# Two attentions of a decoder trunk: raw input for the first, forget gates earlier in the second, and weight low parts added by transfers

## The chip, the cores and the metric

The kernel runs on one core of a Trainium2 chip. The metric is the device time of one execution in microseconds (us); lower is better. Engines are named as the profile names them: PE (TensorE), PEld (its weight loads), DVE (VectorE), ACT (ScalarE), POOL (GpSimd), SP (SyncE). Each engine works through its own queue of instructions strictly in order; a transfer (DMA) is issued by SP or by POOL and runs on 16 shared DMA engines.

## The reference, cut to what matters

The residual stream `x` has 512 tokens of 1024 numbers, 16 heads of 64. There are two layers; each is an attention, a SwiGLU feed-forward and a gated per-layer embedding. Layer 0 uses stick-breaking attention, layer 1 softmax attention with a cumulative forget-gate bias.

```python
def rms_norm(x, g):
    y = xf * lax.rsqrt(jnp.mean(xf * xf, axis=-1, keepdims=True) + EPS)
    return y * g
# layer 0
hn = rms_norm(h, attn_norm_g[0])
q, k, v = split(hn @ sb_w_qkv)
z = einsum('bhqd,bhkd->bhqk', q, k) * scale
w = exp(log_sigmoid(z) + later)      # later: sum of -softplus(z) over the keys between
h = h + merge_heads(w @ v) @ sb_w_o
# layer 1
hs = rms_norm(h, shared_norm_g)
kvf = hs @ shared_w_kvf              # keys, values, 16 forget-gate columns
f_logit = kvf[..., 2 * HD:] + shared_b_f
f_cum = cumsum(log_sigmoid(f_logit), axis=1)
logits = q_normed @ k_normed * scale + f_cum[query] - f_cum[key]
```

The factor of `rms_norm` that belongs to a token (`r` below) can be put in after a product instead of before it, since it is one number for each token.

## The kernel before

**Numbers.** Every float32 operand of a product is held as two `float32r` tiles, a high part and the rest (`wh` and `wl` of a weight, `bh` and `bl` of an activation), and every product is three matmuls: high by high, high by low, low by high (`mm3`, L251 to L253; `by_token`, L397 to L399). The residual stream stays on chip, transposed: `h[0..7]`, each 128 features by 512 tokens.

**Weights.** All weights come from one array in units of 512 KB (128 x 1024), in the order of use. `load_unit` takes a unit: the transfer into `raw` is issued from SP (L136), ACT casts it to `wh` (L153), DVE subtracts to `wl` (`minus`, L126, called from L159). There are two `raw` buffers and four of `wh` and `wl`. `block` loads a unit three units ahead of the one in use (`AHEAD = 3`). A second way for the low part stands in `load_unit` and is not used (`LOW = ("vector", "vector")`): ACT writes the negated rounded weight, and a transfer issued from POOL adds the weight to it in place.

```python
            nc.scalar.copy(wh, raw)
            if state["low"] == "dma":
                nc.scalar.activation(wl, raw, AF.Copy, scale=-1.0)
                nc.gpsimd.dma_start(wl, wall[u], accum_op=ALU.add)
            else:
                minus(wl, raw, wh)
```

**Order of work.** The text of the kernel gives a priority order; a planner at compile time lays out each engine's queue by that priority and by its own estimates of when an operand is ready. `Filler` mixes steps of later projections between the steps of the heads.

**First attention (layer 0).** The input times its gain, not normalised, is put into operand buffer 1 (`ys`, L819). The values of head groups 0 and 1 and the queries and keys of pairs 0 and 1 (`raw_qk`) are computed from it, with `r` put in afterwards. Meanwhile `normalise` (L446) makes the normalised input in operand buffer 0 (`xs`): for each of 8 tiles a DVE product (L449), an ACT cast (L451) and a DVE difference (L126). All later values and pairs (`qk`) use `xs`. For each head, `front` makes the scores `z` on PE, two sigmoids on ACT (L652, L653), a running product and a product on DVE (L655, L658); `back` transposes the weights on PE (L707), copies them as high (ACT, L708) and low part (DVE, L126: `w3l`, `w2l`, `w1l`) and multiplies them with the values (L715). `put` splits queries and keys into high and low (L516, L518), and four transfers issued from POOL swap the halves of the keys (L528).

**Second attention (layer 1).** `group(0)` makes queries and keys of four heads by token. Its two query results wait in PSUM pool `d` (three banks) for `norm_sums` (L225, L228, `newton`), which itself takes a bank of that pool. `norm_bounce` (L241) sends `r` to DRAM (`row`) and reads it back spread over 128 partitions (`rb`). Then `expand(0)` transposes the normalised queries and keys (`qt`, L613), then `forget` computes the gate columns (16 matmuls, `fps`, L477 to L480), multiplies them with `rb` (L484), and goes on over ACT and DVE to `gex`, which is written to DRAM from SP (`gdram`, L497) and read back for each head (`gb`, L639). The first head's softmax needs `gb` (L666).

**End of an attention.** Two partial output projections (`early`, L792) are computed before the last head's output is there.

Of the kernel before, what the change touches and what calls it, by code (L numbers as in the profile page):

```python
# [24 lines left out]
P = 128  # L25
# [60 lines left out]
def trunk(ctx, tc, xT, pT, small, wf, wall, out, dump=None):  # L86
# [277 lines left out]
    def attention(layer, buf):  # L364
# [3 lines left out]
        with tc.tile_pool(name=f"pa{layer}", bufs=1, space=PSUM, reuse_waits="tile") as pa, \  # L368
# [12 lines left out]
            vq = {}  # L381

# [28 lines left out]
            def keep_values(v, r):  # L411
                def emit(t0, ps):
                    src = ps.rearrange("p s (a d) -> p s a d", a=4)
                    if r is None:
                        vh, vl = v[:, t0:t0 + 2, :, 0, :], v[:, t0:t0 + 2, :, 1, :]
                        nc.scalar.copy(vh, src)
                        minus(vl, src, vh)
                    else:
                        for st in range(2):
                            rc = r[:, t0 + st:t0 + st + 1]  # L420
                            vh, vl = v[:, t0 + st, :, 0, :], v[:, t0 + st, :, 1, :]
                            nc.scalar.activation(vh, src[:, st], AF.Copy, scale=rc)
                            nc.vector.scalar_tensor_tensor(vl, src[:, st], rc, vh.bitcast(F32),
                                                           ALU.mult, ALU.subtract)
                return emit
# [5 lines left out]
            if stick:  # L431

                ys = operand(1 - buf)
                held = []
                run(by_token(ys, lambda t0, ps: held.append((t0, ps)), ((0, 1),)))
                m, r = norm_sums(pz, "z")
                keep = keep_values(value_tile(0), r)
                for t0, ps in held:
                    keep(t0, ps)
                v1 = by_token(ys, keep_values(value_tile(1), r))  # L440
                for _ in range(6):
                    next(v1)
                rb = norm_spread(r, pz, "z")
                run(v1)

                def normalise():  # L446
                    for k in range(ND):
                        y = tp.tile([P, S], F32, name="y", tag="ta")
                        nc.vector.scalar_tensor_tensor(  # L449
                            y, h[k], sm[:, G_ATTN[0] + k:G_ATTN[0] + k + 1], rb, ALU.mult, ALU.mult)  # L450
                        nc.scalar.copy(xs[k][0], y)  # L451
                        minus(xs[k][1], y, xs[k][0])
                        yield

                norm = normalise()
# [14 lines left out]
            def forget():  # L470

                fps = ppool["d"].tile([P, S], F32, name="fps", tag="d")
                for k in range(ND):

                    last = k == ND - 1
                    if not last:
                        nc.tensor.matmul(fps[:48], wfs[:, k, :], xs[k][0], start=k == 0, stop=False)  # L477
                    nc.tensor.matmul(fps[:16], wfs[:, k, :16], xs[k][1], start=False, stop=False)
                    if last:
                        nc.tensor.matmul(fps[:48], wfs[:, k, :], xs[k][0], start=False, stop=True)  # L480
                zf = tp.tile([P, S], F32, name="zf", tag="ta")
                nc.scalar.copy(zf[:16], fps[32:48])
                nc.vector.tensor_tensor(zf[:16], zf[:16], fps[:16], ALU.add)
                nc.vector.tensor_tensor(zf[:16], zf[:16], rb[:16], ALU.mult)  # L484
                nc.vector.tensor_scalar_add(zf[:16], zf[:16], sm[:16, C_BF:C_BF + 1])
                ef = tp.tile([P, S], F32, name="ef", tag="ta")
# [4 lines left out]
                gex = tp.tile([P, S], F32, name="gex", tag="ta")[:16]  # L491
# [51 lines left out]
            def raw_qk(p):  # L543

                kb, qb = take(8), take(8)

                def steps(b):
                    g = dense_steps(b, ys)
                    for i in range(ND):
                        try:  # L550
                            next(g)
                        except StopIteration as e:
                            ps = e.value
                        else:
                            if i % 4 == 2:
                                next(norm, None)
                            yield
                    t = tp.tile([P, S], F32, name="qk0", tag="ta")
                    nc.vector.tensor_tensor(t, ps, rb, ALU.mult)
                    next(norm, None)  # L560
                    return t

                yield from put(p, steps(qb), 0.125, steps(kb), 1.0)
                if p == RAW_PAIRS - 1:
                    run(norm)

            qn = {}
            tok = {"r": None}

            def group(g, before=None):  # L570

                for what in "qk":
# [24 lines left out]
                    if what == "q" and before is not None:  # L597
# [3 lines left out]
                        for a in held:  # L601
                            emit(*a)
                    else:
# [29 lines left out]
            def front(hd):  # L633
# [6 lines left out]
                for ti, segs in enumerate(TILES):  # L640
# [102 lines left out]
            if stick:  # L743
                run(raw_qk(0))
            else:
                def sums():
                    m, tok["r"] = norm_sums()

                    tok["em"] = a1.tile([P, 4], F32, name="em")
                    nc.vector.tensor_scalar_mul(tok["em"], m, EPS)  # L750

                run(group(0, sums))
                rb = norm_bounce(tok["r"])
                run(expand(0))
                gdram = forget()
            for e in attn_order(layer)[3 if stick else 2:]:
                i = int(e[1:])
                fill.add(e, (raw_qk(i) if i < RAW_PAIRS else qk(i)) if e[0] == "p" else expand(i) if e[0] == "e" else
# [33 lines left out]
            for n in range(2):  # L792
# [25 lines left out]
    for k in range(ND):  # L818
        emit_x(k, 1, G_ATTN[0], False)  # L819
# [16 lines left out]
LOW = ("vector", "vector")  # L836
# [3 lines left out]
RAW_PAIRS = 2  # L840
# [116 lines left out]
```

## Time and profile before

| | |
|---|---|
| time, median of 3 runs | 1390.91 us (1387.65 to 1391.71) |
| the profiled execution's own time | 1390.78 us |
| span in its trace | 1389.0 us |
| PE busy | 1360.9 us (98%) |
| DVE busy | 814.9 us (59%) |
| ACT busy | 623.8 us (45%) |
| POOL busy | 44.7 us (3%) |
| first attention | about 20 to 268 us of the span |
| second attention | about 700 to 960 us |

The times inside the kernel come from the one profiled execution; its own time is 1.8 us longer than its span. "Busy" of PE counts matmuls that overlap, so full busy does not mean that every cycle is used; the two attentions are the stretches where PE is not fully busy.

### The profile page before, as it was taken

The page shows a single profiled execution, that of the slowest core. Times are in us where ns is not written, and L with a number is a line of the kernel's source. Part 1 is how long each engine was busy: PE and PEld are TensorE (multiplying, and loading weights), DVE is VectorE, ACT ScalarE, POOL GpSimd, SP SyncE. Part 2 cuts the span into 40 slices and gives each one's busy share as a digit, 9 for nine tenths or more (in the row PEclk, how much of TensorE's full clock was granted, in tenths as well). Part 3 has the DMA queues.
Part 4 walks back from the last instruction along what each step waited for, and adds up shares of the span by engine and source line. Part 5 has one row for each costly group of instructions (what it writes and reads, how often), then busy time and mean ns, then how long its engine had stood idle before and what let it go on. Part 6 is the DMA issues. An engine that isn't in the chain of part 4 may idle for free.

```text
span 1389.0 us, 18178 instructions
## 1 busy us (share of the span) xinstructions
PE 1360.9 (98%) x7108; PEld 1151.0 (83%) x7108; DVE 814.9 (59%) x1402; ACT 623.8 (45%) x1086; POOL 44.7 (3%) x95
## 2 busy tenths in 40 slices
PE   7999999999999999999999999999999999999999
PEld 7778877788888888888888999987888888888887
DVE  6898788844444443333867788778454444433335
ACT  6566565623332332322557888777232232322312
POOL 0110010000000000000001101000000000000000
PEclk9999999999999999999999999999999999999999
DMA  5242232333333333332343333332243333333323
GB/s 183 80 118 77 63 105 61 92 85 107 104 91 96 101 93 104 92 97 78 91 117 93 99 92 105 94 99 78 82 122 92 105 91 94 104 91 105 92 70 106
DMA packets 41958, 133.71 MB, mean 96 GB/s; under 512 B 7936, under 2 KB 8320, under 8 KB 41872
## 3 DMA queue, kind: packets, MB, share of 16 engines
q1 hardware_dynamic: 37520, 119.95, 29.3%
q0 software_dynamic: 4352, 12.59, 3.7%
q8 instruction: 56, 0.92, 0.3%
q14 instruction: 30, 0.25, 0.1%
HBM read 121.99 MB, written 2.14 MB: 89 GB/s over the span
## 4 chain that ended last, share of the span: by engine, by line
PE 81%; DVE 8%; ACT 5%; DMA 3%; issue 2%; SPq 0%; ACTq 0%; DVEq 0%; POOLq 0%
PE ps L251 22%; PE ps L253 22%; PE ps L252 22%; PE psv L397 3%; PE psv L398 3%; PE psv L399 3%; PE po L715 3%; PE pt L707 2%; DVE wl L126 2%; DMA row<-r 1%; PE z L624 1%; DVE e L655 1%; PE z L625 1%; ACT wh L153 1%; DVE wl L150 1%
## 5 line engine op out<-in xcount | busy, mean ns | idle before, releaser
L251 PE MATMUL ps<-bh,wh 128*128 128x512 f32 (+1 forms) x1232 | 483.8, 393 | 1.4 <-ACT bh L738 1.4
L253 PE MATMUL ps<-bh,wl 128*128 128x512 f32 (+1 forms) x1232 | 478.7, 389 | 0.0
L252 PE MATMUL ps<-bl,wh 128*128 128x512 f32 (+1 forms) x1232 | 478.1, 388 | 0.0
L153 ACT CAST wh<-raw 128x1024 fp32r<-128x1024 f32 x192 | 201.5, 1050 | 470.5 <-PE ps L252 413.4
L126 DVE TENSOR_TENSOR wl<-raw,wh 128x1024 fp32r<-128x1024 f32 x192 | 234.7, 1223 | 158.7 <-ACT wh L153 158.3
L253 PEld LDWEIGHTS ps<-bh,wl 128*128 128x128 f32 x1232 | 231.5, 188 | 46.8
L251 PEld LDWEIGHTS ps<-bh,wh 128*128 128x128 f32 x1232 | 231.9, 188 | 44.7 <-ACT bh L738 1.9
L252 PEld LDWEIGHTS ps<-bl,wh 128*128 128x128 f32 x1232 | 231.8, 188 | 43.5 <-DVE bl L126 0.4
L397 PE MATMUL psv<-wh,bh 128*128 128x256 f32 x512 | 153.1, 299 | 10.1 <-ACT wh L153 7.0
L398 PE MATMUL psv<-wl,bh 128*128 128x256 f32 x512 | 148.4, 290 | 0.5 <-DVE wl L126 0.5
L399 PE MATMUL psv<-wh,bl 128*128 128x256 f32 x512 | 148.5, 290 | 0.0
L397 PEld LDWEIGHTS psv<-wh,bh 128*128 128x128 f32 x512 | 100.7, 197 | 10.4 <-ACT wh L153 7.0
L294 DVE TENSOR_TENSOR s<-s,ps 128x512 f32<-128x512 f32 x44 | 30.2, 687 | 124.7 <-PE ps L253 124.5
L398 PEld LDWEIGHTS psv<-wl,bh 128*128 128x128 f32 x512 | 100.5, 196 | 1.8 <-DVE wl L126 0.8
L399 PEld LDWEIGHTS psv<-wh,bl 128*128 128x128 f32 x512 | 100.5, 196 | 0.0
L292 DVE TENSOR_TENSOR s<-ps,rb 128x512 f32<-128x512 f32 x44 | 30.2, 691 | 97.5 <-PE ps L253 79.5
L253 PE MATMUL ps<-eh,wl 128*128 128x512 f32 x224 | 87.2, 389 | 0.0
L252 PE MATMUL ps<-el,wh 128*128 128x512 f32 x224 | 87.2, 389 | 0.0
L251 PE MATMUL ps<-eh,wh 128*128 128x512 f32 x224 | 87.2, 389 | 0.0
L707 PE MATMUL pt<-ident,w 128*128 128x128 f32 x320 | 52.7, 276 | 6.2 <-DVE w3l L126 5.1
L624 PE MATMUL z<-ke,qd 128*128 128x256 f32 (+2 forms) x128 | 48.1, 376 | 4.1 <-DVE mx L666 3.1
L707 PEld LDWEIGHTS pt<-ident,w 128*128 128x128 f32 x320 | 38.4, 141 | 15.5 <-DVE w3l L126 8.8
(149 smaller groups left out, 1565.0 us busy)
## 6 DMA issues: line engine op xcount, KB each, us to landing
raw<-in_w_dram SPq DMA_DIRECT2D x216, 512.0 KB, 3.6
kd<-ke POOLq DMA_DIRECT2D x32, 128.0 KB, 2.4
ke<-kd POOLq DMA_DIRECT2D x32, 128.0 KB, 3.3
gb<-gdram POOLq DMA_DIRECT2D x16, 256.0 KB, 3.7
h<-in_x_dram SPq DMA_DIRECT2D x8, 256.0 KB, 5.2
out_dram<-h SPq DMA_DIRECT2D x7, 256.0 KB, 2.0
rb<-row SPq DMA_DIRECT2D x5, 256.0 KB, 4.9
pf<-in_p_dram SPq DMA_DIRECT2D x2, 512.0 KB, 3.9
```

The source lines that it names most:

```text
L126: nc.vector.tensor_tensor(out, a, b.bitcast(F32), ALU.subtract)
L153: nc.scalar.copy(wh, raw)
L251: nc.tensor.matmul(ps, wh, xh, start=first, stop=False)
L252: nc.tensor.matmul(ps, wh, xl, start=False, stop=False)
L253: nc.tensor.matmul(ps, wl, xh, start=False, stop=last)
L292: nc.vector.tensor_tensor(s, g, rb, ALU.mult)
L397: nc.tensor.matmul(ps[:, st], xh, wh, start=first, stop=False)
L398: nc.tensor.matmul(ps[:, st], xh, wl, start=False, stop=False)
L399: nc.tensor.matmul(ps[:, st], xl, wh, start=False, stop=lastk)
L624: nc.tensor.matmul(zt[:, c:c + n], qd[:, t], ke[:, s0:s0 + n], start=True, stop=False)
L707: nc.tensor.transpose(pt[:, bi * P:(bi + 1) * P], blk(j, s), ident)
L715: nc.tensor.matmul(po[:, :m], vv, (tl if low else th)[:, c:c + m], start=gi == 0 and not low, stop=gi == 2 and low)
```

## The change

1. **First attention.** `xs` itself (buffer 0) gets the unnormalised input, and everything is computed from it; `normalise` and `raw_qk` go. Values always get `r` at their evacuation, one ACT and one DVE instruction for each 128 tokens (before, head groups 2 and 3 needed one of each for 256). Keys are multiplied with `rb` on DVE before they are split; queries are split as they are, and the sigmoids take `r/8` and `-r/8` of the query token as their scale, which needs an instruction for each query block, so the third score tile, which holds two blocks, takes two for each sigmoid.
2. **Weights of the first attention.** `LOW` is `("dma", "vector")`: units 7 to 30 get their low parts by the second way shown above.
3. **Second attention.** `norm_sums` takes its PSUM bank from pool `pz`. `sums`, which runs when the queries of `group(0)` are computed and before they are evacuated, also issues `norm_bounce` and the 16 gate matmuls with their first two evacuating instructions; the rest of `forget` follows the evacuation of the queries, ahead of the keys' products. `gdram` is written from POOL instead of SP. `zf`, `ef` and `gex` take buffers of the tag `w`.
4. **End of each attention.** Three partial output projections instead of two.

```diff
@@ keep_values @@
+                    for st in range(2):
+                        rc = r[:, t0 + st:t0 + st + 1]
+                        vh, vl = v[:, t0 + st, :, 0, :], v[:, t0 + st, :, 1, :]
+                        nc.scalar.activation(vh, src[:, st], AF.Copy, scale=rc)
+                        nc.vector.scalar_tensor_tensor(vl, src[:, st], rc, vh.bitcast(F32),
+                                                       ALU.mult, ALU.subtract)
@@ if stick @@
-                ys = operand(1 - buf)
                 held = []
-                run(by_token(ys, lambda t0, ps: held.append((t0, ps)), ((0, 1),)))
+                run(by_token(xs, lambda t0, ps: held.append((t0, ps)), ((0, 1),)))
                 m, r = norm_sums(pz, "z")
+                tok["r"] = r
+                for sign in (1, -1):
+                    tok[sign] = a1.tile([P, 4], F32, name=f"rq{sign + 1}")
+                    nc.vector.tensor_scalar_mul(tok[sign], r, sign * 0.125)
...
-                def normalise():
-                    for k in range(ND):
-                        y = tp.tile([P, S], F32, name="y", tag="ta")
-                        nc.vector.scalar_tensor_tensor(
-                            y, h[k], sm[:, G_ATTN[0] + k:G_ATTN[0] + k + 1], rb, ALU.mult, ALU.mult)
-                        nc.scalar.copy(xs[k][0], y)
-                        minus(xs[k][1], y, xs[k][0])
-                        yield
@@ forget @@
-                zf = tp.tile([P, S], F32, name="zf", tag="ta")
+                zf = a2.tile([P, S], F32, name="zf", tag="w", bufs=WB[layer])
                 nc.scalar.copy(zf[:16], fps[32:48])
                 nc.vector.tensor_tensor(zf[:16], zf[:16], fps[:16], ALU.add)
-                nc.vector.tensor_tensor(zf[:16], zf[:16], rb[:16], ALU.mult)
+                yield
+                nc.vector.tensor_tensor(zf[:16], zf[:16], tok["rb"][:16], ALU.mult)
...
-                nc.sync.dma_start(gdram, gex)
-                return gdram
+                nc.gpsimd.dma_start(gdram, gex)
+                tok["g"] = gdram
@@ qk @@
-                yield from put(p, dense_steps(qb, xs), 0.125, dense_steps(kb, xs), 1.0)
+                def keys():
+                    ps = yield from dense_steps(kb, xs)
+                    t = tp.tile([P, S], F32, name="kr", tag="ta")
                     nc.vector.tensor_tensor(t, ps, rb, ALU.mult)
                     return t
+                yield from put(p, dense_steps(qb, xs), 1.0, keys(), 1.0)
@@ group @@
                         before()
                         for a in held:
                             emit(*a)
+                        run(after)
@@ front @@
-                        nc.scalar.activation(e[:, :n], z, AF.Sigmoid, scale=-1.0)
-                        nc.scalar.activation(w[:, :n], z, AF.Sigmoid)
+                        for out, sign in ((e, -1), (w, 1)):
+                            for j, c, m in segs:
+                                nc.scalar.activation(out[:, c:c + m], z[:, c:c + m], AF.Sigmoid,
+                                                     scale=tok[sign][:, j:j + 1])
@@ the second attention's start @@
                 def sums():
-                    m, tok["r"] = norm_sums()
+                    m, tok["r"] = norm_sums(pz, "z")
                     tok["em"] = a1.tile([P, 4], F32, name="em")
                     nc.vector.tensor_scalar_mul(tok["em"], m, EPS)
-                run(group(0, sums))
-                rb = norm_bounce(tok["r"])
+                    tok["rb"] = norm_bounce(tok["r"])
+                    next(gates)
+                gates = forget()
+                run(group(0, sums, gates))
+                gdram = tok["g"]
                 run(expand(0))
-                gdram = forget()
@@ ends @@
-            for n in range(2):
+            for n in range(3):
-        emit_x(k, 1, G_ATTN[0], False)
+        emit_x(k, 0, G_ATTN[0], False)
-LOW = ("vector", "vector")
+LOW = ("dma", "vector")
```

## Rows read from the trace of the kernel before

**Rows 1.** Busy time by engine in stretches: us (instructions), clock, DMA share, GB/s.

```profile
core 0: us, PE busy (x) PEld busy (x) DVE busy (x) ACT busy (x) POOL busy (x), PEclk, DMA share, GB/s
20.00:268.00 248.00, 239.44 (x1364) 197.10 (x1363) 209.22 (x332) 147.01 (x263) 16.65 (x32) 1.00 0.31 87
700.00:705.00 5.00, 2.29 (x17) 2.20 (x16) 4.18 (x14) 4.34 (x11) 0.00 (x0) 0.82 0.41 129
705.00:710.00 5.00, 5.00 (x25) 5.00 (x25) 3.69 (x23) 0.67 (x5) 0.00 (x0) 0.50 0.26 82
...
745.00:750.00 5.00, 5.00 (x31) 4.37 (x31) 2.66 (x11) 4.01 (x11) 0.57 (x1) 0.75 0.55 161
```

**Rows 2.** Waits of PE, 20 to 268 us: total us, times, longest.

```profile
PE pt L707 <- DVE w3l L126: 5.1, 5, 1.3
PE po L715 <- DVE w1l L126: 1.0, 1, 1.0
```

**Rows 3.** DVE in order of time around one of these waits: start, us.

```profile
140.68 1.22 DVE L126 TENSOR_TENSOR wl<-raw,wh 128x1024 fp32r<-128x1024 f32 x1
...
143.35 0.69 DVE L126 TENSOR_TENSOR w3l<-pt,w3h 128x512 fp32r<-128x512 f32 x1
```

**Rows 4.** Groups on DVE, 20 to 268 us: count, busy us, mean ns, idle before.

```profile
L126 DVE TENSOR_TENSOR wl<-raw,wh 128x1024 fp32r<-128x1024 f32 x31 | 37.9, 1223 | 7.7 <-ACT wh L153 7.5
...
L449 DVE SCALAR_TENSOR_TENSOR y<-h,sm,rb 128x512 f32<-128x512 f32 x8 | 5.9, 749 | 0.0
L126 DVE TENSOR_TENSOR bl<-y,bh 128x512 fp32r<-128x512 f32 x8 | 5.5, 688 | 0.4 <-ACT bh L451 0.2
```

**Rows 5.** Groups on ACT, 20 to 268 us.

```profile
L153 ACT CAST wh<-raw 128x1024 fp32r<-128x1024 f32 x31 | 32.5, 1049 | 22.1 <-PE ps L252 13.8 <-DMA raw<-in_w_dram 4.9 <-PE psv L399 3.3
L653 ACT ACTIVATE w<-z 128x384 f32<-128x384 f32 x32 | 15.9, 498 | 0.0
```

**Rows 6.** Transfers issued, 20 to 268 us: count, KB each, median us to landing.

```profile
raw<-in_w_dram SPq DMA_DIRECT2D x31, 512.0 KB, 3.7
```

**Rows 7.** Groups on POOL, 20 to 268 us.

```profile
L528 POOL DMA_DIRECT2D ke<-kd x16 | 8.3, 517 | 5.6 <-DVE kd L518 3.8 <-issue 1.7
```

**Rows 8.** Casts of weight units 7 and 10 on ACT: start, us.

```profile
36.81 1.04 ACT L153 CAST wh<-raw 128x1024 fp32r<-128x1024 f32 x1
...
57.50 1.05 ACT L153 CAST wh<-raw 128x1024 fp32r<-128x1024 f32 x1
```

**Rows 9.** PE in order of time at the second attention's start.

```profile
703.89 0.58 PE L397 MATMUL psv<-wh,bh 128*128 128x256 f32 x1 [2.71 <-DVE m L228]
...
718.31 0.48 PE L477 MATMUL fps<-bh,wfs 128*48 128x512 f32 x1
...
722.10 0.28 PE L397 MATMUL psv<-wh,bh 128*128 128x256 f32 x1
...
742.95 0.41 PE L624 MATMUL z<-ke,qd 128*128 128x384 f32 x1 [2.45 <-DVE mx L666]
```

**Rows 10.** SP's queue in order of time, the same stretch.

```profile
709.06 0.43 SPq L244 DMA_DIRECT2D row<-r  x1
719.42 0.33 SPq L246 DMA_DIRECT2D rb<-row  x1
```

**Rows 11.** DVE in order of time, the same stretch.

```profile
721.94 0.69 DVE L593 TENSOR_TENSOR qn<-psv,r 128x512 f32<-128x512 f32 x1
...
724.46 0.68 DVE L484 TENSOR_TENSOR zf<-zf,rb 16x512 f32<-16x512 f32 x1 [0.87 <-DMA rb<-row]
```

**Rows 12.** DVE in order of time, layer 0's embedding gate.

```profile
654.86 0.69 DVE L331 TENSOR_TENSOR s<-ps,rb 128x512 f32<-128x512 f32 x1 [13.14 <-DMA rb<-row]
655.47 1.22 DVE L126 TENSOR_TENSOR wl<-raw,wh 128x1024 fp32r<-128x1024 f32 x1
```

**Rows 13.** ACT in order of time, the same stretch.

```profile
646.16 1.05 ACT L153 CAST wh<-raw 128x1024 fp32r<-128x1024 f32 x1 [8.06 <-PE ps L252]
```

**Rows 14.** Waits of PE, 940 to 960 us.

```profile
PE ps L251 <- ACT bh L738: 1.4, 1, 1.4
```

More of the change, by code (lines that the diff above doesn't have):

```diff
@@ L381, in attention @@
             vq = {}
+            tok = {}
             def by_token(xs, emit, halves=((0,), (1,))):
@@ L413, in emit @@
                     src = ps.rearrange("p s (a d) -> p s a d", a=4)
[L414 to L424, printed above, removed]
+                    for st in range(2):
[4 more added lines that the diff above has]
+                                                       ALU.mult, ALU.subtract)
                 return emit
@@ L439, in attention @@
                     keep(t0, ps)
-                v1 = by_token(ys, keep_values(value_tile(1), r))
+                v1 = by_token(xs, keep_values(value_tile(1), r))
                 for _ in range(6):
@@ L444, in attention @@
                 run(v1)
-                def normalise():
-                    for k in range(ND):
-                        y = tp.tile([P, S], F32, name="y", tag="ta")
-                        nc.vector.scalar_tensor_tensor(
-                            y, h[k], sm[:, G_ATTN[0] + k:G_ATTN[0] + k + 1], rb, ALU.mult, ALU.mult)
-                        nc.scalar.copy(xs[k][0], y)
-                        minus(xs[k][1], y, xs[k][0])
-                        yield
-                norm = normalise()
             oh, ol = bh[1 - buf], bl[1 - buf]
@@ L480, in forget @@
                         nc.tensor.matmul(fps[:48], wfs[:, k, :], xs[k][0], start=False, stop=True)
-                zf = tp.tile([P, S], F32, name="zf", tag="ta")
+                zf = a2.tile([P, S], F32, name="zf", tag="w", bufs=WB[layer])
                 nc.scalar.copy(zf[:16], fps[32:48])
                 nc.vector.tensor_tensor(zf[:16], zf[:16], fps[:16], ALU.add)
-                nc.vector.tensor_tensor(zf[:16], zf[:16], rb[:16], ALU.mult)
+                yield
+                nc.vector.tensor_tensor(zf[:16], zf[:16], tok["rb"][:16], ALU.mult)
                 nc.vector.tensor_scalar_add(zf[:16], zf[:16], sm[:16, C_BF:C_BF + 1])
-                ef = tp.tile([P, S], F32, name="ef", tag="ta")
+                ef = a2.tile([P, S], F32, name="ef", tag="w", bufs=WB[layer])
                 nc.scalar.activation(ef[:16], zf[:16], AF.Abs)
@@ L490, in forget @@
                 nc.vector.scalar_tensor_tensor(zf[:16], zf[:16], 0.0, ef[:16], ALU.min, ALU.subtract)
-                gex = tp.tile([P, S], F32, name="gex", tag="ta")[:16]
+                gex = a2.tile([P, S], F32, name="gex", tag="w", bufs=WB[layer])[:16]
                 nc.vector.tensor_tensor_scan(gex, zf[:16], zf[:16], 0.0, ALU.add, ALU.bypass)
@@ L540, in qk, with group @@
                 kb, qb = take(8), take(8)
-                yield from put(p, dense_steps(qb, xs), 0.125, dense_steps(kb, xs), 1.0)
[L543 to L558, printed above, removed]
+                def keys():
+                    ps = yield from dense_steps(kb, xs)
+                    t = tp.tile([P, S], F32, name="kr", tag="ta")
                     nc.vector.tensor_tensor(t, ps, rb, ALU.mult)
-                    next(norm, None)
                     return t
-                yield from put(p, steps(qb), 0.125, steps(kb), 1.0)
-                if p == RAW_PAIRS - 1:
-                    run(norm)
+                yield from put(p, dense_steps(qb, xs), 1.0, keys(), 1.0)
             qn = {}
-            tok = {"r": None}
-            def group(g, before=None):
+            def group(g, before=None, after=None):
                 for what in "qk":
@@ L743, in attention @@
             if stick:
-                run(raw_qk(0))
+                run(qk(0))
             else:
                 def sums():
-                    m, tok["r"] = norm_sums()
+                    m, tok["r"] = norm_sums(pz, "z")
                     tok["em"] = a1.tile([P, 4], F32, name="em")
                     nc.vector.tensor_scalar_mul(tok["em"], m, EPS)
-                run(group(0, sums))
-                rb = norm_bounce(tok["r"])
+                    tok["rb"] = norm_bounce(tok["r"])
[3 more added lines that the diff above has]
+                gdram = tok["g"]
                 run(expand(0))
-                gdram = forget()
             for e in attn_order(layer)[3 if stick else 2:]:
                 i = int(e[1:])
-                fill.add(e, (raw_qk(i) if i < RAW_PAIRS else qk(i)) if e[0] == "p" else expand(i) if e[0] == "e" else
+                fill.add(e, qk(i) if e[0] == "p" else expand(i) if e[0] == "e" else
                          group(i) if e[0] == "g" else values(i, tok["r"]))
@@ L839 @@
 WB = (6, 4)
-RAW_PAIRS = 2
 PIN = (0, 0)
```

## The prediction, made blind

> **What bounds the kernel now.** I read the table of stretches first: in the feed-forward PE is busy all the time at full clock, so nothing that is done beside it there can pay. Only the two attentions leave PE idle. In the first one, 20 to 268 us, PE is busy 239.44 of 248 us, so at most 8.6 us are to be had; DVE is busy 209 us (84%) and ACT 147 us (59%) [rows 1]. The list of PE's waits says which engine ends the idle time: six waits for low parts of the transposed weights, 6.1 us in all, none over 1.3 us [rows 2]. The order of time on DVE shows why: `w3l` starts at 143.35, behind the 1.22 us of a weight unit's low part that began at 140.68 [rows 3]. The low part itself is not what PE misses; it stands in the queue ahead of what PE misses.
>
> At the start of the second attention PE stands twice: 2.71 us until 703.89, since the first keys' products need a bank that the sums of squares hold until DVE has read them, and 2.45 us until 742.95, where the first head waits for the gates [rows 9]. After each, the granted clock is at the lower of its two levels (1.2 GHz) for a while: 0.50 over 705 to 710 and 0.75 over 745 to 750 [rows 1]. At half speed from 703.89 to about 710 it loses 3.0 us of work, and 5 x 0.25 = 1.3 us the second time. That start costs 2.7 + 3.0 + 2.5 + 1.3 = 9.5 us. At the end of the second attention PE stands 1.4 us for the last head's output [rows 14].
>
> **The first attention, part by part.** DVE loses 24 unit low parts of 1.223 us (units 7 to 30; 29.4 us) and the eight products and differences of `normalise`, 5.9 + 5.5 us [rows 4]. It gains four key products more than the four it had, at the 0.69 us of a product of that shape [rows 12], 2.8 us, and about 1 us for values evacuated in halves: 209 - 37 = 172 us, 69%. The two scaled copies of `r` are four columns wide and I cost them at nothing: PE has the second value group's products beside them.
>
> ACT gains 24 negated copies. A cast of that width takes 1.049 us: 25.2 us. A cast of 384 columns takes 0.498, so 640 columns more cost 0.551 and what does not depend on the width is about 0.498 - 384 x 0.551 / 640 = 0.17 us [rows 5]. By it the 32 sigmoids that become two each cost 5.4 us more, and the eight casts of `normalise` that go save 8 x 0.61 = 4.9 us. With 1 us for the values: 147 + 27 = 174 us, 70%. Both engines then have a third of their time free.
>
> The six waits should go: each is at most 1.3 us, and 1.22 us of low part goes from the queue ahead. Bounds: nothing (ACT's copy delays the high parts as DVE's did the low ones) and 8.6 us (no idle time left). I take 5.5 of the 6.1 us, since the copy that feeds `w3l` can now stand behind 1.05 us more of ACT.
>
> **The accumulating transfers.** None runs before. Nearest below is the plain transfer of the same unit, 3.7 us to landing [rows 6]; far above lies a transfer of scattered words, `row`, which took 10.4 us from its issue until SP could issue the next on it [rows 10]. It reads the old contents as well, so I take twice the plain one, 7.4 us. There is room for either bound: unit 7 is cast at 36.81 and unit 10 at 57.50; a unit is loaded when the one three before it comes into use, so unit 7 is needed about 20.7 us after its cast begins [rows 8]. Less two ACT instructions of 1.05 us, 18.6 us remain. In volume: 0.31 of the engines move 87 GB/s [rows 1], so all of them some 281 GB/s and a plain unit takes 1.9 us of all sixteen; 24 at twice that are 90 us beside the 77 us in use, of 248. Cost: nothing.
>
> On POOL the 24 issues at 0.52 us [rows 7] are 12 us beside 16.65 us [rows 1]. Behind an issue that waits for its ACT copy stand the key swaps of the next pair (and who waits for those is PE's `z`); the copy and the keys' split come from ACT in the same order, so I cost this at nothing too.
>
> This is the place where a rule speaks against the change. The row: the 16 issues took 0.517 us each while DVE was 84% busy, so nothing was held up. The Trainium skill (SBUF — State Buffer, "SBUF: two separate sides") says that a transfer issued from GpSimd needs GpSimd to write its descriptors, and that certain VectorE instructions lock it out for their whole length; its example goes from about 0.62 to 3.1 us. By that, an estimate from the page is 24 x 2.5 = 60 us more on POOL's queue, which POOL's idle time still covers; by the row it is nothing.
>
> **The start of the second attention.** The sums of squares get their own bank. The 16 gate matmuls, 718.31 to 722.10, 3.8 us [rows 9], move to about 701.2, so they fill the first wait and more. But they take the third bank themselves: it is free after an ACT copy and a DVE addition, some 1.6 us, or PE waits for the queries' evacuation. So PE stands 1.6 us at about 705, and I assume that the clock holds, as at the wait of 1.4 us [rows 14]. The keys' products took from 703.89 to 718.31 with 3.0 us lost to the clock, so 11.4 us: they end at about 718, as before.
>
> Now the moved step waits. `rb` is issued earlier in the text, but it leaves when `r` is there: `row` at 709.06, `rb` in use at 724.46, 15.4 us later [rows 10, 11]. How early does the planner expect it? At layer 0's embedding gate DVE stands 13.14 us for `rb`, from 641.7; behind it in the queue stands a weight low part whose cast ended at 647.2 [rows 12, 13]. So the planner expects `rb` within 5.5 us. For the changed kernel that is by 714.6, ahead of the second half of the keys, which DVE finishes normalising at 722.6 [rows 11]. The gates' product with `rb` now has priority over the keys, so DVE should stand until 724.4 with the keys queued behind it, and PE behind them with the transposes. After 724.4 come the product and the bias, 1.2 us; the keys' own chain took 718.31 to 722.6, 4.3 us, of which a little, the squares on ACT, is done by then, so I take 3.8: 729.4. PE stands from 722 to 729.4, 7.4 us, and pays 3.0 us of clock again. The gates reach DRAM no later than before, and the keys are by then the later ones, so the 2.45 us at 742.95 go, with their clock. Sum: 1.6 + 7.4 + 3.0 = 12.0 against 9.5, a loss of 2.5 us. Bounds: a gain of 9.5 - 1.6 = 7.9 (nothing stands), a loss of 7 (all that ACT and DVE put off comes first, keys at 734). I take 2.5, by the four rows of the gate.
>
> `gdram` on POOL costs nothing by itself: the issue of 0.52 us replaces one on SP. What it may hold up is the first pair's key swaps behind it.
>
> **The end.** The third partial projection is 9 matmuls; 16 took 3.8 us, so 2.1 us, more than the 1.4 it has to fill. Gain 1.4; below, nothing, if the third bank is late.
>
> **Sum.** The profiled execution took 1390.78 us (span 1389.0), and the median is 1390.91, 0.1 us above. 1390.8 - 5.5 - 1.4 + 2.5 = 1386.4 us.
>
> **The rivals.**
> A. The gates don't block. The planner puts the keys first, or `rb` comes in time. PE then stands only 1.6 us, and the first head still waits 2.5 + 1.3: 5.4 against 9.5. 1390.8 - 5.5 - 1.4 - 4.1 = 1379.8. For it: the keys' evacuation and `rb` are close in the planner's eyes. Against: rows 12.
> B. ACT takes DVE's place in the first attention: 27 us more on a queue that already stands 22.1 us before its casts [rows 5]. Gain there 1 instead of 5.5: 1390.9.
> C. The whole backlog of the start comes first: loss 7, 1390.9.
> D. Slower: the accumulating transfers are the bound. Place: the 16 engines, units 7 to 30. They have 248 - 77 = 171 us free, so it decides from 7.1 us of all sixteen engines a unit, almost four times a plain one. At 8 us the 24 units need 21 us more than there is, the gain of the first attention is gone, and 1390.8 - 1.4 + 2.5 + 21 = 1413. For it: nothing in the trace but that the operation is unseen; against: the factor. The rule on descriptors would add to it if the key swaps in the same queue came late; the trace gives that a chance of 2 in 100, and it is in D's.
>
> **Chances.** Forecast 0.45, own range 1382 to 1391; A 0.25; B 0.11; C 0.10; D 0.09. About 0.3% (4.2 us) can be told from no change: faster means below 1386.7. The forecast's range lies around that bound, a little over half of it faster (0.25), the rest the same; A is faster; B the same; C the same or a little slower (0.06 slower); D slower. Faster 0.50, same 0.35, slower 0.15. The range 1377 to 1395 leaves out D and the outer ends of A and C.
>
> **What would show it.** First attention: no waits for `w3l`, DVE near 172 us and ACT near 174 us; casts and copies in pairs; accumulating transfers landing in 4 to 10 us. Second: gate matmuls at about 1 us after the sums, PE standing under 2 us there at full clock; then DVE standing some 10 us for `rb` with keys behind it, and PE standing at the transposes. If DVE normalises the keys before it stands, A is right. If PE waits for `wl` by a transfer, D is. The prediction is wrong most easily by the planner's new order, which no row of the old kernel shows.

## The result, and the profile after

The changed kernel took 1401.64 us (median of 4, 1400.21 to 1402.95); the kernel before, on the same chip, 1389.77 (median of 4). The ratio is 1.0086, 95% interval 1.0069 to 1.0103: slower, where 1386.4 was forecast, and outside the range. The span of the profiled execution is 1400.2 us against 1389.0.

**Where the time went.** Each of the norms begins with the first matmul of `ssq` (the sums of squares), so these five times cut the span: 23.4, 288.4, 644.3, 706.1 and 990.6 us (before: 22.9, 282.5, 638.4, 700.2 and 979.5). The first attention, between the first two, took 265.0 us (259.6 before), +5.4; the second, between the last two, 284.5 (279.3), +5.3; before the first there are 0.5 us more. The rest agrees. 5.4 + 5.3 + 0.5 = 11.2, the whole difference of the spans. Both attentions lost, so at least two steps of the prediction failed.

Busy time by stretch, the view of [rows 1] (engines as there: PE, PEld, DVE, ACT, POOL; then clock, DMA share, GB/s):

```profile
20.00:268.00 248.00, 236.65 (x1342) 194.87 (x1341) 171.06 (x293) 173.04 (x308) 38.51 (x56) 0.99 0.60 136
40.00:60.00 20.00, 16.48 (x72) 12.90 (x71) 7.56 (x12) 9.74 (x16) 3.92 (x6) 0.91 0.82 184
60.00:80.00 20.00, 15.35 (x76) 11.61 (x75) 11.56 (x22) 12.85 (x23) 3.92 (x6) 0.97 0.57 117
...
736.10:746.10 10.00, 6.96 (x38) 6.96 (x39) 6.24 (x19) 2.71 (x7) 3.23 (x6) 0.58 0.58 176
```

The busy time of DVE and ACT came out as worked out, 171 and 173 us for a forecast of 172 and 174. Yet PE is busy 2.8 us less than in [rows 1]. It loses 6.1 us from 40 to 80 us, where the DMA engines are 82% and then 57% busy, and gains 3.3 us elsewhere. The same two stretches in the kernel before:

```profile
40.00:60.00 20.00, 18.75 (x93) 14.36 (x92) 17.55 (x26) 13.67 (x25) 2.21 (x4) 1.00 0.38 105
60.00:80.00 20.00, 19.16 (x98) 15.17 (x97) 19.84 (x34) 12.31 (x22) 3.09 (x6) 1.00 0.35 93
```

PE's waits, the view of [rows 2], 20 to 268 us, then at the second attention's start (695 to 760) and end (940 to 975, the counterpart of [rows 14]):

```profile
PE z L597 <- DMA ke<-kd: 7.5, 2, 4.0
PE pt L682 <- DVE w3l L126: 2.7, 5, 0.9
...
PE qt L586 <- DVE qn L565: 8.6, 1, 8.6
PE psv L398 <- DVE u L212: 2.4, 1, 2.4
...
PE ps L251 <- ACT bh L713: 1.3, 1, 1.3
```

`w3l` still ends five waits, though they shrank from 5.1 to 2.7 us; a new wait of 7.5 us has come, two times, for `ke`: the key swap, a small transfer on chip that puts keys into the other half of the partitions. The transfers issued, the view of [rows 6], 20 to 268 us, with the share of the software queue (packets, MB, share of 16 engines):

```profile
q0 software_dynamic: 4992, 16.78, 35.0%
...
raw<-in_w_dram SPq DMA_DIRECT2D x30, 512.0 KB, 4.3
wl<-in_w_dram POOLq DMA_DIRECT2D x24, 512.0 KB, 7.8
kd<-ke POOLq DMA_DIRECT2D x16, 128.0 KB, 4.6
ke<-kd POOLq DMA_DIRECT2D x16, 128.0 KB, 5.7
```

POOL's queue and PE in order of time at the first of the two waits:

```profile
44.57 0.87 POOL L157 DMA_DIRECT2D wl<-in_w_dram  x1 [5.30 <-ACT wl L156]
45.13 0.87 POOL L518 DMA_DIRECT2D kd<-ke  x1
45.79 0.75 POOL L518 DMA_DIRECT2D ke<-kd  x1
46.33 0.72 POOL L518 DMA_DIRECT2D kd<-ke  x1
46.83 0.72 POOL L518 DMA_DIRECT2D ke<-kd  x1
51.38 0.93 POOL L157 DMA_DIRECT2D wl<-in_w_dram  x1 [3.82 <-ACT wl L156]
...
54.08 0.47 PE L597 MATMUL z<-ke,qd 128*128 128x512 f32 x1 [3.52 <-DMA ke<-kd]
```

The accumulating transfer took 7.8 us to landing; 7.4 was the estimate. What it does to its neighbour was not in the sum: the swap of 45.79 is used at 54.08, 8.3 us later. The four `ke` swaps issued over 36 to 75 us, in the kernel before and in the changed one (the last number is the median time to landing):

```profile
ke<-kd POOLq DMA_DIRECT2D x4, 128.0 KB, 3.1
...
ke<-kd POOLq DMA_DIRECT2D x4, 128.0 KB, 8.4
```

In the second attention, DVE in order of time, as [rows 11], with PE's entries as [rows 9] and SP's as [rows 10]:

```profile
714.41 0.47 DVE L150 SCALAR_TENSOR_TENSOR wl<-raw,sm,wh 128x256 fp32r<-128x256 f32 x1
729.27 0.68 DVE L474 TENSOR_TENSOR zf<-zf,rb 16x512 f32<-16x512 f32 x1 [14.39 <-DMA rb<-row]
729.88 0.67 DVE L553 TENSOR_REDUCE mm<-sqn 128x8 f32<-128x512 f32 x1
...
736.80 0.67 DVE L553 TENSOR_REDUCE mm<-sqn 128x8 f32<-128x512 f32 x1
...
740.21 0.69 DVE L565 TENSOR_TENSOR qn<-psv,r 128x512 f32<-128x512 f32 x1
...
706.94 0.43 PE L466 MATMUL fps<-bh,wfs 128*48 128x512 f32 x1
...
713.23 0.35 PE L398 MATMUL psv<-wh,bh 128*128 128x256 f32 x1 [2.37 <-DVE u L212]
...
739.14 0.69 PE L586 MATMUL qt<-ident,qn 128*128 128x128 f32 x2 [8.59 <-DVE qn L565]
...
714.51 0.38 SPq L244 DMA_DIRECT2D row<-r  x1
725.28 0.33 SPq L246 DMA_DIRECT2D rb<-row  x1
```

The gate matmuls start 0.8 us after the sums, as forecast. Then DVE stands 14.4 us for `rb` with the keys' reduction (729.88) queued behind it, and PE stands 8.6 us for the keys. Over 736 to 746 us the clock that was granted is 0.58.

### The profile page after: what moved, and what is told of

Same layout as the page of the kernel before. It is cut to its first block, busy times and chain, and to the rows that moved or that the text cites. A ratio compares the mean times of both kernels' runs of the same rounds, so it can differ in the third digit from the quotient of the medians.

```text
span 1400.2 us, 18267 instructions
## 1 busy us (share of the span) xinstructions
PE 1363.5 (97%) x7108; PEld 1152.7 (82%) x7108; DVE 782.1 (56%) x1372; ACT 654.2 (47%) x1138; POOL 67.2 (5%) x120
## 4 chain that ended last, share of the span: by engine, by line
PE 80%; DVE 8%; ACT 6%; DMA 4%; issue 2%; POOL 0%; SPq 0%; DVEq 0%; ACTq 0%
PE ps L251 21%; PE ps L252 21%; PE ps L253 21%; PE psv L399 3%; PE psv L400 3%; PE psv L398 3%; PE po L690 3%; PE pt L682 2%; DMA row<-r 1%; PE z L597 1%; DMA ke<-kd 1%; PE z L598 1%; DVE e L630 1%; DVE wl L126 1%; DVE wl L150 1%
## 5 line engine op out<-in xcount | busy, mean ns | idle before, releaser
L126 DVE TENSOR_TENSOR wl<-raw,wh 128x1024 fp32r<-128x1024 f32 x168 | 205.3, 1222 | 153.8 <-ACT wh L153 153.5
L630 DVE TENSOR_TENSOR_SCAN e<-e 128x512 f32<-128x512 f32 (+1 forms) x64 | 50.8, 815 | 13.2 <-ACT e L627 12.8
```

The lines of the kernel that those rows point to most:

```text
L126: nc.vector.tensor_tensor(out, a, b.bitcast(F32), ALU.subtract)
L630: nc.vector.tensor_tensor_scan(e[:, c:c + m], e[:, c:c + m], e[:, c:c + m], 1.0, ALU.mult, ALU.bypass)
```

## The experiments

All times are medians; each ratio is to the kernel before, timed on the same chip. "First" and "second" are the lengths of the two attentions, cut as above, each from one profiled execution. Three kernels with the same first attention gave 264.2 to 266.4 (the changed kernel, gates later, `rb` spread by PE), so 2 us of such a length can be scatter where the swaps are late. Where they are not, kernels with the same first attention agree within 0.6 us. Four kernels with the second attention of the changed kernel gave 282.4 to 285.4.

| kernel | time, us | ratio (interval) | first | second |
|---|---|---|---|---|
| before | 1389.77 | | 259.6 | 279.3 |
| changed | 1401.64 | 1.0086 (1.0069 to 1.0103) | 265.0 | 284.5 |
| low parts on DVE | 1396.67 | 1.0058 (1.0043 to 1.0073) | 261.2 | 282.4 |
| plain transfers instead | 1396.97 | 1.0056 (1.0043 to 1.007) | 260.7 | 284.2 |
| swaps on SP | 1398.39 | 1.0071 (1.0056 to 1.0086) | 261.4 | 285.4 |
| gates later in the text | 1400.68 | 1.0085 (1.0068 to 1.0102) | 266.4 | 283.9 |
| `rb` spread by PE | 1391.53 | 1.0012 (1.0001 to 1.0023) | 264.2 | 274.7 |
| both: DVE and PE | 1387.99 | 0.999 (0.9982 to 0.9999) | 261.0 | 275.2 |
| accumulating from the third head on, `rb` by PE | 1384.59 | 0.9967 (0.9955 to 0.998) | 258.9 | 275.7 |
| the same, two partials | 1384.73 | 0.9965 (0.9953 to 0.9978) | 258.3 | 274.4 |
| before, accumulating | 1390.60 | 1.0012 (1.0003 to 1.0022) | 260.0 | 280.2 |
| before, `rb` spread | 1390.32 | 1.001 (0.9998 to 1.0022) | 259.6 | 277.3 |
| old first, new second | 1386.08 | 0.9975 (0.9966 to 0.9984) | 259.6 | 273.6 |
| the same, accumulating from the third head on | 1384.65 | 0.9965 (0.9953 to 0.9978) | 257.8 | 274.8 |

### First attention: the accumulating transfers

**Low parts on DVE again**, nothing else changed.

```diff
-LOW = ("dma", "vector")
+LOW = ("vector", "vector")
```

> The changed kernel with one thing undone: the low parts of the first attention's weights come from VectorE again. The first feed-forward's sums of squares, at 282.6 us before and 288.5 us after, mark the end of the first attention. Theory 1 (the key swaps queue behind the accumulating transfers of GpSimd): the two waits of PE for the swaps, 7.5 us, go with their clock, the gain from the unnormalised input stays, the mark comes at 278 to 282 us and the time is 1391 to 1395. Rival (the scaled sigmoids and ScalarE's longer queue cost the time): the mark stays near 288 and the time near 1400.

The mark, the end of the first attention, came at 284.2 us and the time was 1396.67, both above what theory 1 gave and below its rival. The first attention took 261.2. So 3.8 of its 5.4 us go with the transfers, and 1.5 us with the input that is not normalised. PE's waits show `w3l` back at 5.3 us and `ke` down to one of 1.8.

**The same bytes, not accumulated.** DVE makes the low parts, and where the accumulating transfer stood a plain one of the same unit overwrites the raw copy, which nobody reads any more.

```diff
-                nc.scalar.activation(wl, raw, AF.Copy, scale=-1.0)
-                nc.gpsimd.dma_start(wl, wall[u], accum_op=ALU.add)
+                minus(wl, raw, wh)
+                nc.gpsimd.dma_start(raw, wall[u])
```

> The changed kernel with its low parts on DVE again, and on POOL, in the place of each accumulating transfer, a plain transfer of the same unit from DRAM over the raw copy that it was cast from (the same bytes, nothing accumulated; its values are not used). V (the traffic itself makes the first key swaps late, whatever it does on landing): the swaps of the first pairs land after 7 to 9 us, PE waits for them 5 to 8 us over 20 to 268 us, first attention 264 to 266, median 1400 to 1402. A (it is the accumulation: twice the work on the engines for each packet): the swaps land after 4 to 5 us, PE waits for them under 2.5 us, first attention 261 to 262.5, median 1396 to 1398. The share of the queue's packets against the accumulating kernel's 33% of 260 us gives the price of accumulation by itself.

Waits of PE and transfers issued over 20 to 288 us, the stretch from 40 to 60 us, the transfers issued over 36 to 75 us, and POOL in order of time:

```profile
PE pt L682 <- DVE w3l L126: 5.4, 7, 1.1
PE z L597 <- DVE qd L508: 1.0, 1, 1.0
...
q0 software_dynamic: 4992, 16.78, 21.5%
...
raw<-in_w_dram POOLq DMA_DIRECT2D x24, 512.0 KB, 4.1
...
40.00:60.00 20.00, 18.14 (x90) 13.89 (x90) 13.27 (x18) 11.93 (x24) 3.19 (x6) 1.00 0.62 184
...
ke<-kd POOLq DMA_DIRECT2D x4, 128.0 KB, 3.4
...
44.90 0.52 POOL L518 DMA_DIRECT2D ke<-kd  x1 [0.20 <-issue]
45.54 0.57 POOL L157 DMA_DIRECT2D raw<-in_w_dram  x1
```

No wait for `ke` is left and the first attention is that of the kernel without the transfers. From 40 to 60 us it moves as many GB/s as the changed kernel, 184, at a DMA share of 0.62 instead of 0.82. The queue's packets take 21.5% of the 16 engines' time over 20 to 288 us, those of the changed kernel 32.4%, with 4992 packets and 16.78 MB in both; the swaps alone are 5.7% (the kernel with low parts on DVE). So a plain unit costs (0.215 - 0.057) x 268 / 24 = 1.8 us of all sixteen engines and an accumulating one 3.0, 1.7 times as much. For the same bytes, accumulating takes the engines longer. The median, 1396.97, is the one that A gave.

That accumulation by itself makes the swaps late is not shown, because this edit also changed the order of issue. In the changed kernel the accumulating transfer of 44.57 is issued just ahead of the swaps; here the plain one, at 45.54, stands behind them. The changed kernel's own later swaps show what the order does. From 100 us on, POOL issues them ahead of the accumulating transfer:

```profile
107.45 0.52 POOL L518 DMA_DIRECT2D ke<-kd  x1
107.99 0.95 POOL L157 DMA_DIRECT2D wl<-in_w_dram  x1
```

These 20 swaps landed in 2.1 to 6.5 us and PE waits for none of them, though the DMA engines are 65% busy from 100 to 240 us. The 12 before them, issued up to 2.5 us behind a plain load and an accumulating transfer, took 6.5 to 8.8 us. Plain loads delay swaps too: in the kernel before, swaps with no load ahead or close behind took a median of 2.2 us, those issued up to 2.5 us behind one load 4.6. By these rows two plain loads ahead would give some 7 us (2.2 + 2 x 2.4), an estimate; no run tried it, nor the accumulating transfers with the first swaps issued ahead of them.

**The swaps on SP's queue.**

```diff
-  nc.gpsimd.dma_start(a[i][other[i]].bitcast(F32), b[i][mine[i]].bitcast(F32))
+  nc.sync.dma_start(a[i][other[i]].bitcast(F32), b[i][mine[i]].bitcast(F32))
```

> The changed kernel with the key swaps issued from SP instead of GpSimd; the accumulating transfers stay. Theory 1 (order within one queue): the swaps land in 2 to 5 us although the accumulating transfers run, PE waits under 1 us for them, the mark comes at 279 to 284 us, the time is 1392 to 1397. Rival 1b (the 16 engines themselves are full): the swaps still take about 8 us at 45 and 69 us, and the mark stays at 287 or later. A third way: SP stands on the swaps and the weights come late behind them, which the waits for raw would show.

PE in order of time, and the transfers issued over 36 to 75 us:

```profile
54.11 0.47 PE L597 MATMUL z<-ke,qd 128*128 128x512 f32 x1 [3.25 <-DMA ke<-kd]
...
ke<-kd SPq DMA_DIRECT2D x4, 128.0 KB, 7.4
```

Issued at 45.83 from a queue with no accumulating transfer, the swap is as late as before. The accumulating transfer was issued just ahead of it, at 44.88 from POOL. The waits for `ke` fell only from 7.5 to 5.3 us, so the place in POOL's queue is the smaller part; by this the rest lies on the sixteen engines, which both queues share. In this run the software queue holds nothing but accumulating transfers, 26.9% of the engines' time over 20 to 288 us, which again is 3.0 us for a unit. The time, 1398.39, lies between theory 1 and its rival. Its first attention, 261.4, is better than the waits say, and that is left open.

**The accumulating transfers on the kernel before**, from unit 7 on, with its own normalised input.

```diff
-LOW = ("vector", "vector")
+LOW = ("dma", "vector")
```

> The kernel before with only the low parts of the first attention's weights from accumulating transfers. Theory 1: the swaps of the first pairs land in about 8 us instead of 3 to 4 and PE waits for them, partly hidden since this kernel reaches the first scores later; later waits for w3l shrink; first attention 259 to 264 us, time 1389 to 1394. Rival (the loss needs the unnormalised input): no wait for swaps, first attention 255 to 258, time 1385 to 1388.

They make the swaps late here too: waits for `ke` of 3.7 us, DMA share 0.76 over 40 to 60 us. `w3l` fell from 5.1 to 1.9 us, and over 100 to 240 us PE is busy 138.7 instead of 136.8 us. The gain of the later part pays for the loss of the earlier: 260.0 against 259.6.

**Accumulating only from the third head on**, with `rb` spread by PE as below. Since units are loaded ahead of their use, the first accumulating transfer is that of 90.66 us, after the swaps of three pairs, and 18 units accumulate instead of 24.

```diff
-            state["low"] = LOW[layer]
...
+                    if hd == 2:
+                        state["low"] = LOW[layer]
```

> rb by PE, and the low parts from accumulating transfers only from the third head on, after the key swaps of the first two pairs. Theory 1 as it stands (the transfers hurt only where the swaps are needed at once, at 45 to 80 us): PE waits under 2 us for swaps, the later stretch keeps its shorter idle time, the first attention is 257 to 260 us and the time 1381 to 1385. Rival (the unnormalised input itself costs, or the transfers crowd the engines everywhere): 261 us or more from mark to mark and 1387 or more.

The first attention took 258.9, against 261.0 with low parts on DVE and 264.2 with all accumulated. So accumulating the later 18 units is worth 2 us, and accumulating the first six as well costs 5.

### Second attention: the moved gates

**Gates later in the text**, behind the transposes of the first group.

```diff
-                run(group(0, sums, gates))
-                gdram = tok["g"]
-                run(expand(0))
+                run(group(0, sums, iter(())))
+                run(expand(0))
+                run(gates)
+                gdram = tok["g"]
```

> The changed kernel with the rest of the gates, from their product with rb on, put behind the first pair's transposes, as before; the gate matmuls stay early. Theory 2 (VectorE stands for rb with the keys behind it): the wait of 8.6 us for the normalised keys goes, the way from the first feed-forward's mark to the end falls from 1111.7 us to 1104 to 1108, the time is 1394 to 1398. Rival (the bank that the early gate matmuls take, and their place on PE, cost the time): PE still stands there and the time stays above 1400.

DVE in order of time:

```profile
729.05 0.68 DVE L474 TENSOR_TENSOR zf<-zf,rb 16x512 f32<-16x512 f32 x1 [14.49 <-DMA rb<-row]
729.66 0.67 DVE L553 TENSOR_REDUCE mm<-sqn 128x8 f32<-128x512 f32 x1
```

Theory 2 was not tested, since the product did not move: it comes later in the text than the keys and is still queued ahead of them, and PE still waits 8.7 us. So it is not the text's priority: the planner must expect `rb` to be there before the keys.

**`rb` spread by PE and ACT** instead of two transfers, all else as changed.

```diff
-                    tok["rb"] = norm_bounce(tok["r"])
+                    tok["rb"] = norm_spread(tok["r"], pz, "z")
```

> The changed kernel with rb of the second attention spread by PE (as the first attention does) instead of the two transfers over DRAM; the order of the text is unchanged. Theory 2: the product with rb waits 2 to 3 us after r and not 15, the 8.6 us of PE go, the gates are in DRAM by 722 and the first head starts early; from the first feed-forward's mark to the end 1100 to 1105 us instead of 1111.7, the time 1390 to 1395. Rival (order and bank): above 1398.

DVE in order of time, and PE's waits from 695 to 760 us:

```profile
716.65 0.68 DVE L474 TENSOR_TENSOR zf<-zf,rb 16x512 f32<-16x512 f32 x1 [3.24 <-ACT rb L238]
...
729.56 0.69 DVE L565 TENSOR_TENSOR qn<-psv,r 128x512 f32<-128x512 f32 x1
...
PE psv L398 <- DVE u L212: 2.2, 1, 2.2
PE qt L586 <- DVE qn L565: 0.2, 1, 0.2
```

DVE stands 3.2 us, while the keys are not there yet, and PE's wait of 8.6 us is gone. The second attention took 274.7, 9.8 less than changed and 4.6 less than before.

**The kernel before with only that edit.**

> The kernel before with one thing changed: rb of the second attention is spread by TensorE and an ACT copy in place of the two DMAs; gates, first attention and partials as before. S1 (what the changed kernel lost at the start of the second attention is the DMA path of rb, and the gate products that moved up gain by themselves): the second attention from 279.2 to 276 to 278 us, the wait of 2.5 us for the gates before the first head stays, median 1386 to 1388. S2 (the spreading alone brings the whole gain, the order of the gates is worth nothing): 273 to 275 us, median 1383 to 1385. S3 (rb was hidden before, so nothing changes): 279 us, 1389 to 1390.

The second attention took 277.3. This kernel's eleven times lie between 1387.84 and 1395.28, and their median shows no gain, so the 2 us of the profile are not confirmed by the time. All kernels together give four cases for the second attention:

| | `rb` by transfer | `rb` by PE |
|---|---|---|
| gates late | 279.3 and 280.2 | 277.3 |
| gates early | 282.4 to 285.4 (4 kernels) | 273.6 to 275.7 (6 kernels) |

By the means the moved gates lose 4.4 us with the transfers and gain 2.6 with PE; the gain hangs on the one profile of 277.3.

**Two partial projections instead of three**, on the kernel with accumulation from the third head on.

```diff
-            for n in range(3):
+            for n in range(2):
```

> The kernel with rb spread and accumulating low parts from the third pair on, but two early partials as before instead of three. If the third partial filled the wait of 1.4 us at the end, this kernel is 1.4 to 2 us slower than with three (1384.6), 1386; if the planner only runs the partials earlier and the wait stays, the time is 1384 to 1385 and the end of the second attention differs by under 0.5 us.

1384.73 against 1384.59, and PE's waits from 940 to 975 us are the same with two as with three:

```profile
PE ps L251 <- ACT bh L713: 1.3, 1, 1.3
```

The third partial is worth nothing.

### Put together

**Low parts on DVE and `rb` by PE**, both edits above at once.

> Both repairs on the changed kernel: low parts from VectorE and rb of the second attention spread by PE. If the two losses are independent, the first attention is 261 us from mark to mark (as with the low parts from VectorE alone) and the rest 1102 us: about 1386.5 us, 0.2 to 0.3% faster than before. If the shorter second attention of the other run came from an earlier or quieter state that the first attention left behind, the sum fails and the time is 1389 or more.

1387.99 lies between the two expectations, 1.5 us above the sum. The first attention of 261.0 and the second of 275.2 are near the 261.2 and 274.7 that each edit gave alone, so the two losses are separate as far as the profiles show. With both undone the kernel is about level with the one before, 0.999.

**The first attention of before, the second of the changed kernel** with `rb` by PE; and the same with accumulating low parts from the third head on.

> The first attention as it was before (normalised input, low parts from VectorE), with the changed second attention, rb by PE and three early projections. Theory 2: first attention 259.6 us, the rest 1102, time 1384.5 to 1386.5. If the gain of the rest needs what the changed first attention leaves, 1389 or more.

> The first attention of the kernel before with accumulating low parts from the third pair of heads on, and the new second attention with rb spread by TensorE and three early partials. If the parts add up: first attention 256 to 258 us (before 259.6; normalised input saves 1.5 us against the run with unnormalised input and the same late start, 258.9), second 273.5 us, median 1380 to 1383. If the accumulating transfers only pay where DVE has the halved values and the key products to do: first attention 259 to 260, median 1385 to 1387.

1386.08, and 1384.65 us. The first attention of the former is 259.6, so the input that is not normalised costs 1.5 us (261.0 and 261.2 with it). With the late accumulation it is 257.8, 1.8 us better. The median of this last kernel came out above the 1380 to 1383 that the sum of parts gave, and can't be told from 1384.59 of the kernel that keeps the unnormalised input. Busy time and PE's waits, 20 to 268 us, of this last kernel:

```profile
20.00:268.00 248.00, 241.42 (x1367) 198.42 (x1367) 191.51 (x316) 164.81 (x283) 33.08 (x50) 1.00 0.52 127
...
PE pt L709 <- DVE w3l L126: 3.1, 5, 0.9
PE po L717 <- DVE w1l L126: 1.0, 1, 1.0
```

No wait for `ke`, full clock, and PE busy 2.0 us more than in [rows 1]. This kernel is faster than both the kernel before and the changed one; against the kernel before the ratio is 0.9965, interval 0.9953 to 0.9978.

## Why the prediction was wrong

**The key swaps, costed at nothing: the step that failed first.** "Behind an issue that waits for its ACT copy stand the key swaps of the next pair" named the right place, but asked only whether they would be issued late. They were issued in time and landed late, 8.4 us instead of 3.1, and cost 7.5 us of waits, with a granted clock of 0.91 and 0.97 in those stretches. The runs show that the accumulating transfers do it: without them the wait is 1.8 us, with them only from 90 us on 1.6, and in the kernel before they bring a wait of 3.7 where there was none. Whether accumulation matters there, or only a second large transfer issued just ahead of the swaps, stays open: in the run with plain transfers, which has no such wait, these stand behind the swaps.

**The volume of the transfers.** 7.4 us to landing was right (7.8), and so was the room of 18.6 us: no wait of PE is for `wl`. Twice the plain unit's time on the engines was a little high (1.7 times). Rival D was rightly refused by its volume over 248 us, 0.60 of the engines' time. That mean hid the stretch that counts: units 7 to 9 meet the first swaps at a share of 0.82. The bound of the range, all 16 engines full, was the wrong one; a small transfer on the path suffers before that, by what is issued just ahead of it.

**The rule on descriptors.** POOL's issues of accumulating transfers took 0.902 us on average instead of the 0.517 of [rows 7], and plain ones 0.551. The Trainium skill (SBUF — State Buffer, "SBUF: two separate sides") lays such delays to certain VectorE instructions that lock GpSimd out of writing descriptors. Here DVE was less busy than before, 69%, and the issues lengthened with the kind of transfer. No issue took the 2.5 us more that the prediction drew from its example; which of DVE's instructions here are of that kind no run shows.

**The first attention's gain of 5.5.** The busy times were right, the gain was mis-sized. `w3l` fell only to 2.7 us, and where nothing else disturbs, accumulation is worth 1.8 us in the old kernel and 2 to 3 in the new. Taking 1.22 us of low part off DVE's queue did not shorten what stands ahead of `w3l` otherwise: at the wait of 0.67 us that ends at 65.11, DVE went from a scan (62.71) through the product `w` (63.77) straight to `w3l` (64.36). The normalisation, worth 11.4 us of DVE's time, was on nobody's path, and without it PE lost 1.5 us. Where that falls was not tried. Two of the kernels with DVE low parts have one wait for `ke` of 1.4 and 1.8 us, but the one with plain transfers has none and still took 260.7, so that wait does not explain it.

**The start of the second attention.** The mechanism was right: DVE stood for `rb`, keys behind it, PE behind them; `rb` came 23.2 us after the sums, against 24.2 in the forecast. PE's first wait was 2.4 instead of 1.6 us. What was mis-sized is the time from there to the keys' end, 1.2 + 3.8 us in the sum. They ended at 740.9, 11.6 us after `rb`: DVE and ACT had put off eight quarters of weight units (`wl`, 0.47 us each on DVE), and these and the gates' own chain came in between. That is the backlog of rival C: 34.8 us after the sums instead of the 29.2 forecast, and C had put it at 33.8. The wait of 2.45 us for the gates went, as said. Over the 60 us after the sums PE is busy 48.8 us, 54.0 before.

**The end.** The 1.4 us did not go: the wait is 1.3 us. The planner runs the partials earlier, and the last head's output ends the same wait.

**The sum.** First attention -5.5 forecast, +5.4 found; second +2.5 - 1.4 = +1.1 forecast, +5.3 found. The two misses, 10.9 and 4.2, are 15.1 us; 1386.4 + 15.1 = 1401.5. With the 0.5 us ahead of the first norm, which nobody forecast, it is 1402.0, and the profiled execution took 1402.09.

## What to carry to other kernels

A mean share of the DMA engines says nothing of the stretch where a small transfer sits on the path: look for that stretch and for what is issued just ahead of the small one, and ask what the new traffic does to the landing of its neighbours, not only whether it arrives in time itself. Before a step that waits for a transfer is moved ahead, see whether the planner knows how long the transfer takes; if it does not, the step blocks its engine, and everything put off meanwhile comes before the work that was waiting. The same move can lose or gain with the way its operand is made: here it lost 4.4 us with the one, and with the other gained 2.6 by the profiles.

## What the hardware showed

An accumulating transfer of 512 KB from DRAM took 7.8 us to landing against 3.6 to 4.1 for a plain one, 1.7 times the engines' time, and 0.90 us to issue from POOL against 0.55. On-chip transfers of 128 KB landed by what was issued ahead of them. In the kernel before, they took 2.1 to 2.6 us with no load ahead or close behind, and 3.5 to 5.3 up to 2.5 us behind a plain load of 512 KB. In the changed kernel they took 6.5 to 8.8 us behind a plain load and an accumulating transfer, and 6.0 to 8.3 when issued from SP (to 90 us). Issued ahead of the accumulating transfer they took 2.1 to 6.5 us, with the DMA engines 65% busy.
